# One hybrid attention and RWKV layer: the compressed branch's weights laid out as diagonal blocks of a 128x512 tile, in two parts

## The chip, the core and the metric

The kernel runs on one core of a Trainium2 chip. A core has several engines that run side by side, each with a queue of its own that it takes in order: TensorE (PE) multiplies matrices, its weight loads stand as PEld in the profile; VectorE (DVE), ScalarE (ACT) and GpSimd (POOL) work elementwise; SyncE (SP) starts most transfers, which 16 DMA engines carry out. Operands lie in SBUF with 128 partitions, and PE writes its results to PSUM. The metric is device time in microseconds (us) of one execution; less is better.

## What is computed

One layer on 512 tokens of 1024 features: an input projection, two mixers side by side (attention with three branches, and an RWKV7 recurrence), an output projection, and a feed-forward part. The change concerns the first of the three attention branches, the compressed one: keys and values of blocks of 32 tokens, one every 16, are each made into one compressed key and value, 31 of them. Cut to it, the reference reads:

```python
def query_block(q0):                      # 64 queries
    s_c = jnp.einsum('bqhgd,bnhd->bhgqn', qb, kc) - m[:, :, None, None] * d_c
    p_c = softmax_masked(s_c, d_c >= 0)
    o_c = jnp.einsum('bhgqn,bnhd->bqhgd', p_c, vc)     # n: 31 compressed values
    ...                                   # o_s: selected blocks, o_w: sliding window
    o = gb[..., 0:1] * o_c + gb[..., 1:2] * o_s + gb[..., 2:3] * o_w

# in the layer
x = x + jnp.concatenate([y_nsa, y_rwkv], axis=-1) @ w_out[l]
hidden = jnp.square(jax.nn.relu(rmsnorm(x, ln_ffn_g[l]) @ w_ff1[l]))
x = x + hidden @ w_ff2[l]
```

There are 8 query heads of 64 features, in two groups of four that share a key and value head.

## The kernel before

**Two-part numbers.** Most products are made from numbers split in two: a high part of the type fp32r (float32r), copied and rounded by ACT, and a low part, the remainder, subtracted by DVE (`split`, lines 311 and 312: `whi`, `wlo`). Products of such parts are single instructions of up to 512 columns. A plain product of two f32 operands stands in the trace as two matmul records.

**Units of attention.** The tokens lie in four tiles of 128. Attention is done in eight units, one for each pair of a key and value head g and a token tile i, g = 0 first, i from 0 to 3 in each. `attn_scores(i, g)` first makes the scores of the compressed branch for four heads (`pcs`, L1050), their exponentials, and divides them by their sum and multiplies by the gate; the result is `pcm`, 128 tokens by 4 heads x 32 blocks. Then it does the same with the two other branches over `w` = 128 (i + 1) keys (`sc`, products at L1072, DVE at L1076, ACT behind it, the tile is `P`). At the end PE transposes `pcm` (`pct`, L1089): row 32 h + n now holds the weights of head h for block n, with the tokens in the columns, and ACT copies it to SBUF (`pcT`, L1091). `attn_values(i, g)` goes through the key tiles of the two other branches in steps; a step transposes the four heads' weights (`pT`, L1108), splits them (`th` by ACT, L1112; `tl` by DVE, L1113) and multiplies the two parts with the values (`pv`, L1121 and L1125), 512 columns each, all into one PSUM tile. The first step also adds the compressed branch, one product for each head, in plain f32:

```python
if m == 0:
    for h in range(4):
        PE.matmul(pv[0:64, h * 128:(h + 1) * 128], VCM[:, g, h, :], pcT, start=False, stop=False)
```

`VCM[:, g, h, :]` is 128 x 64 and holds the compressed values in the rows 32 h to 32 h + 31 and zeros elsewhere (memset by POOL at L906), so that each product picks its head out of `pcT`. `tb` (L1129) and two adds then bring the unit's result into `YN`. The transposes `pct` and `pT` share a PSUM place "pb" with two buffers.

**What lies beside it.** The recurrence runs as other streams at the same time: `Tn` (L694) and `pz` (L681, L702) belong to the inverse of triangular matrices in blocks of 32, `QL` (L654) and `QD` (L963) are copies and splits on DVE, the chain over blocks of 64 tokens has the products `pp` and `puu` (64 columns), and at its end `py` (L752 to L755, 64 columns), from which `Sn` (L760), the new state, is made; `pty`, `rs_yo` and `Y` belong to the recurrence's output, `ptb` and `puu` to its preparation, `pq` transposes queries, and `kkn`, `mk` are elementwise products on the recurrence's keys. `wo_load` brings in `w_out`, the weights of the output projection, in two halves of eight tiles: each is loaded to one of two buffers (`wraw`, place 'wr'), copied by ACT (`whi`) and subtracted by DVE or POOL (`wlo`). The second half begins when the last unit's scores are made. `outproj` multiplies (`pa`, L332 to L334) as soon as the results of all units of a token tile are split. After that comes the feed-forward part (`pw`, `po`), which the change does not touch.

**What sets the order.** The streams are Python generators. Each yields the time that a step takes on PE and a delay, or a condition on what other streams have done; `merge` takes the stream of the best priority that is ready. The program written so is then handed to a scheduler that orders the instructions of each engine once more by its own model of their times. A changed instruction can therefore move others far from it, on all engines. Tiles in SBUF come from named places with a fixed number of buffers; a step waits for the buffer that it takes.

Of the kernel before, what the change touches and what calls it, by code (L numbers as in the profile page):

```python
# [16 lines left out]
# T tokens in NT tiles, D features in KD tiles; the rest orders the streams of work and their loads  # L17
T = 512
# [40 lines left out]
# places in SBUF: size of each in bytes, and how many  # L59
# [8 lines left out]
# columns of the constant array  # L68
# [46 lines left out]
def layer(ctx: ExitStack, tc: tile.TileContext, A, cst, out):  # L115
# [7 lines left out]
    # ------------------------------------------------------------- scheduling  # L123
    # Work is written as streams: a stream yields (time on the tensor engine, delay until what it
    # waits for is there), or a condition on the other streams, and the streams are merged by that.
# [30 lines left out]
    # ------------------------------------------------------------------ pools  # L156
# [24 lines left out]
    def cycle(*places):  # L181
        """Allocation that goes round some places."""
        k = [0]

        def f(shape, name, dt=F32):
            k[0] += 1
            return at(places[(k[0] - 1) % len(places)], shape, name, dt)
        return f
# [4 lines left out]
    # -------------------------------------------------------------- constants  # L193
# [15 lines left out]
    def gain_load(src, place):  # L209
        """Gains per feature, in all partitions."""  # L210
# [37 lines left out]
    # vectors that are used per feature, 128 features to a row  # L248
# [49 lines left out]
    # ---------------------------------------------------------------- helpers  # L298
    def rsqrt(v, n, key, p=128):
        """1/sqrt of a small array of positive numbers."""  # L300
# [6 lines left out]
    def split(raw, shape, hi=None, lo=None, eng=V):  # L307
        """A matrix in two parts, which add up to it exactly."""
# [27 lines left out]
    def norm_T(i, x_, gain, NH_, NL_, place, pool, raw=None):  # L336
        """Token tile i, normed, into the features' layout, in two parts."""
# [17 lines left out]
    # ------------------------------------------------------------ input norm  # L355
# [5 lines left out]
    def xk(k, i0=0, i1=NT):  # L361
        """The rows of a group of features, for tokens tiles i0 to i1."""
        return XH[k // 4][:, i0:i1, k % 4, :], XL[k // 4][:, i0:i1, k % 4, :]
# [6 lines left out]
    # =============================================================== RWKV  # L370
# [30 lines left out]
    # blocks of projected columns in the order of their use  # L401
# [6 lines left out]
    def turn_of(n):  # L408
        """A part of the input products waits for the one before it."""
# [10 lines left out]
    def raw_piece(p_):  # L420
        """A piece before it is split."""
# [6 lines left out]
    def piece(c0, h):  # L428
        """The next piece of the input weights; those after it are on their way."""
# [13 lines left out]
    def feat_cols(c0, use, halves=False):  # L443
        """Two tiles of 128 projected columns, features in the partitions."""
# [83 lines left out]
    def rw_prep(i):  # L528
# [49 lines left out]
        # products of keys with queries  # L578
# [26 lines left out]
    def rw_vals(i):  # L605
# [3 lines left out]
        # values, tokens in the partitions: odd heads in rows 0-63, even ones in rows 64-127  # L609
# [9 lines left out]
        # the bonus takes the place of the values in their other layout  # L619
# [25 lines left out]
    def rw_inv(i):  # L645
# [3 lines left out]
        # inverse of the triangular matrices: blocks of 32, merged from 2 up  # L649
# [162 lines left out]
    # =============================================================== NSA  # L812
# [7 lines left out]
    VCM = cp.tile([128, 2, 4, 64], F32, name="VCM")  # L820
# [3 lines left out]
    def nsa_consts():  # L824
        # gains of the keys, with those of the queries and the scale
# [7 lines left out]
    def tok_cols(c0, n, use):  # L833
        """Projected columns, tokens in the partitions."""
# [12 lines left out]
    def compress(kind, ckv):  # L847
        """Compressed keys (0) or values (1)."""
# [56 lines left out]
        else:  # L905
            G.memset(VCM, 0.0)  # L906
            for h in range(4):
                G.tensor_copy(VCM[32 * h:32 * h + 32, :, h, :], cm)
# [6 lines left out]
    def keys(b, kb):  # L915
        """Keys of branch b: normed, in two parts, transposed."""
# [55 lines left out]
    def nsa_in():  # L972
# [4 lines left out]
        def cmp_in(j, pa):  # L977
            """Each token's features with those of the next one below them."""
# [451 lines left out]
```

## Time and profile before

| | |
|---|---|
| device time, median of 3 runs | 816.68 us (814.18 to 823.08) |
| the profiled execution: span | 818.9 us, 18281 instructions; nothing is given outside the span |
| PE busy | 797.5 us, 97% of the span |
| PEld (weight loads, beside PE) busy | 684.4 us, 84% |
| DVE busy | 511.0 us, 62% |
| ACT busy | 395.9 us, 48% |
| POOL busy | 174.1 us, 21% |
| DMA | 62.00 MB, mean 76 GB/s |

The profiled execution is one run under the hardware profiler, recorded from its first to its last instruction. An engine's busy time counts the instructions that it carries out; PE's matmuls are pipelined, so a PE that is busy all the time is not one that runs at its peak. [...]

### The profile page before, as it was taken

Reading aid. Unit: us, or ns where it says so; the run is one execution under the profiler, and the core shown is the slowest. Engines: PE = TensorE matmul, PEld = TensorE weight load, DVE = VectorE, ACT = ScalarE, POOL = GpSimd, SP = SyncE. Lnnn points to the kernel's source line nnn. Section 1 sums busy time; section 2 is a strip of 40 time slices with the busy share of each in tenths; the row PEclk is TensorE's granted clock in tenths of the full one; section 3 lists DMA queues with packets and bytes.
Section 4 is the critical chain, followed back from the end, with each engine's and each line's share of the span. In section 5 each row is a group of like instructions: output and inputs, shape, how many; then the busy total and the mean of one; then the engine's idle time right before and its main releaser. Section 6 shows DMA issues by size and latency. Waiting matters only on the chain.

```text
span 818.9 us, 18281 instructions
## 1 busy us (share of the span) xinstructions
PE 797.5 (97%) x7357; PEld 684.4 (84%) x7357; DVE 511.0 (62%) x1157; ACT 395.9 (48%) x928; POOL 174.1 (21%) x176
## 2 busy tenths in 40 slices
PE   7999999999989999999999999999999999999998
PEld 5888888988878787887777889998888999978886
DVE  6344385674575399488764699986333799963333
ACT  6343334345353476569643564675332366663320
POOL 4002042312241252344320024310001323100000
PEclk9999999999975799599999999999999999999999
DMA  6741321120000000020134223314332343133212
GB/s 225 207 116 52 79 80 56 29 54 14 3 15 1 28 3 2 1 68 15 40 103 117 90 77 108 102 51 142 99 98 88 114 117 104 59 111 114 90 52 103
DMA packets 67338, 62.00 MB, mean 76 GB/s; under 512 B 6013, under 2 KB 53299, under 8 KB 67254
## 3 DMA queue, kind: packets, MB, share of 16 engines
q1 hardware_dynamic: 67254, 60.83, 24.9%
q8 instruction: 58, 0.95, 0.5%
q14 instruction: 26, 0.21, 0.1%
HBM read 58.72 MB, written 2.10 MB: 74 GB/s over the span
## 4 chain that ended last, share of the span: by engine, by line
PE 79%; DVE 11%; ACT 4%; DMA 3%; issue 2%; SPq 1%; POOL 0%; DVEq 0%; ACTq 0%; POOLq 0%
PE pa L332 7%; PE pa L333 7%; PE pa L334 7%; PE po L332 7%; PE po L333 7%; PE po L334 7%; PE pw L333 4%; PE pw L334 4%; PE pw L332 3%; PE sc L1072 3%; PE pg L586 2%; DVE wlo L312 2%; PE py L754 2%; PE py L752 2%; DMA wraw<-in_w_out_dram 2%
## 5 line engine op out<-in xcount | busy, mean ns | idle before, releaser
L311 ACT CAST whi<-wraw 128x512 fp32r<-128x512 f32 (+1 forms) x128 | 78.7, 622 | 141.5 <-PE po L333 29.1
L312 DVE TENSOR_TENSOR wlo<-wraw,whi 128x512 fp32r<-128x512 f32 (+1 forms) x120 | 86.2, 721 | 93.6 <-ACT whi L311 87.8
L332 PE MATMUL po<-whi 128*128 128x512 f32 x256 | 100.6, 394 | 1.6 <-DVE cc L1358 1.6
L333 PE MATMUL po<-wlo,whi 128*128 128x512 f32 x256 | 101.0, 395 | 0.0
L334 PE MATMUL po<-whi,wlo 128*128 128x512 f32 x256 | 100.7, 393 | 0.0
L333 PE MATMUL pw<-TT,whi 128*128 128x256 f32 x224 | 63.2, 282 | 0.0
L334 PE MATMUL pw<-TT,wlo 128*128 128x256 f32 x224 | 63.0, 281 | 0.0
L332 PE MATMUL pw<-TT,whi 128*128 128x256 f32 x224 | 62.5, 279 | 0.0
L332 PEld LDWEIGHTS po<-whi 128*128 128x128 f32 x256 | 48.0, 188 | 13.5 <-ACT whi L311 2.0
L334 PEld LDWEIGHTS po<-whi,wlo 128*128 128x128 f32 x256 | 48.1, 188 | 11.4
L333 PEld LDWEIGHTS po<-wlo,whi 128*128 128x128 f32 x256 | 48.1, 188 | 11.0
L332 PE MATMUL pa<-XH,whi 128*128 128x512 f32 (+1 forms) x144 | 53.6, 377 | 1.0 <-ACT XH L350 1.0
L333 PE MATMUL pa<-XL,whi 128*128 128x512 f32 (+1 forms) x144 | 54.4, 379 | 0.0
L334 PE MATMUL pa<-XH,wlo 128*128 128x512 f32 (+1 forms) x144 | 53.5, 374 | 0.0
L1086 POOL TENSOR_SCALAR P<-P,z 128x128 f32<-128x128 f32 (+3 forms) x32 | 35.6, 1122 | 77.9 <-DVE z L1035 35.5
L1288 POOL TENSOR_TENSOR ws<-wq 128x512 f32<-128x512 f32 x14 | 21.5, 1533 | 138.4 <-DMA wq<-in_w_ff_dram 123.4
L312 DVE TENSOR_TENSOR wlo<-ws,whi 128x512 fp32r<-128x512 f32 x56 | 48.1, 870 | 3.1 <-ACT whi L311 3.0
L311 ACT CAST whi<-ws 128x512 fp32r<-128x512 f32 x56 | 33.0, 618 | 34.8 <-PE pw L334 10.0
L312 DVE TENSOR_TENSOR wlo<-H,whi 128x512 fp32r<-128x512 f32 x32 | 22.1, 689 | 42.3 <-PE po L333 32.7
L334 PE MATMUL pw<-NH,wlo 128*128 128x256 f32 x168 | 47.0, 280 | 0.0
L333 PE MATMUL pw<-NL,whi 128*128 128x256 f32 x168 | 46.8, 279 | 0.0
L332 PE MATMUL pw<-NH,whi 128*128 128x256 f32 x168 | 46.8, 279 | 0.0
(319 smaller groups left out, 2109.8 us busy)
## 6 DMA issues: line engine op xcount, KB each, us to landing
wraw<-in_w_ff_dram SPq DMA_DIRECT2D x72, 256.0 KB
wq<-in_w_ff_dram SPq DMA_DIRECT2D x56, 256.0 KB
wraw<-in_w_in_dram SPq DMA_DIRECT2D x40, 256.0 KB
wraw<-in_w_in_dram SPq DMA_DIRECT2D x8, 268.0 KB
x<-in_x_dram SPq DMA_DIRECT2D x8, 256.0 KB
y<-in_x_dram SPq DMA_DIRECT2D x8, 256.0 KB
wraw<-in_w_out_dram SPq DMA_DIRECT2D x8, 256.0 KB
wraw<-in_w_out_dram SPq DMA_DIRECT2D x16, 128.0 KB
```

What stands on the lines that cost most here:

```text
L311: S.copy(hi, raw)
L312: eng.tensor_tensor(lo, raw, hi.bitcast(F32), op=ALU.subtract)
L332: PE.matmul(o_, l[0], r[0], start=first, stop=False)
L333: PE.matmul(o_, l[0], r[1], start=False, stop=False)
L334: PE.matmul(o_, l[1], r[0], start=False, stop=last)
L586: PE.matmul(pg[:, f], BK[ROW[e], 2 * f + c].rearrange("p a b -> p (a b)"), AR[c][ROW[e], f].rearrange("p a b -> p (a b)"), start=True, sto ...
L752: PE.matmul(py[ROW[1 - e], 1, f, :], AR[c][ROW[e], f, 1, :], S_[ROW[e], f, :], start=True, stop=False)
L754: PE.matmul(py[ROW[1 - e], 1, f, :], YL[e][c][:, f, 1 - e, :], uv, start=not q, stop=True)
L1072: PE.matmul(sc[:, h - h0, :], Qt[:, h, :], KT[br, g, hl].rearrange("p i t -> p (i t)")[:, 0:w], start=hl == 0, stop=hl == 1)
L1086: (G if (h, br) in SCG else V).tensor_scalar(P_[:, h, 0:w], P_[:, h, 0:w], z[:, h:h + 1], None, op0=ALU.mult)
L1288: G.tensor_tensor(s3, q[0][0], q[1][0], op=ALU.subtract)
```

## The change

The four plain products become two products of parts. `VCM` now holds the compressed values of a head in all four groups of 32 rows, its high part in columns 0 to 63 and its low part in columns 64 to 127. The weights take the shape of diagonal blocks: a tile `PCD` of 128 x 512 has the weights of head h in the rows 32 h to 32 h + 31 and the columns 128 h to 128 h + 127, and zeros elsewhere, one tile for the high part and one for the low. There are two such pairs, which the units take in turn; they are set to zero once, by POOL, and only the blocks are written after that: for each head one ACT copy of 32 rows by 128 from `pct` and one DVE subtract. The values' low part thus reaches the rows 64 to 127 of `pv`, which are added to the rows 0 to 63 at the unit's end as before. The program is also built with a smaller scratch area for DMA descriptors, 8192 bytes, and comments are dropped, so line numbers move by up to 12.

```diff
@@ -817,12 +817,15 @@
-    VCM = cp.tile([128, 2, 4, 64], F32, name="VCM")
+    VCM = cp.tile([128, 2, 2, 64], F32R, name="VCM")
+    PCD = [[cp.tile([128, 4, 128], F32R, name=f"PCD{n}{hl}") for hl in range(2)] for n in range(2)]
...
@@ -903,9 +906,14 @@
-            G.memset(VCM, 0.0)
+            v4 = at('cs', [128, 2, 64], "v4")
             for h in range(4):
-                G.tensor_copy(VCM[32 * h:32 * h + 32, :, h, :], cm)
+                G.tensor_copy(v4[32 * h:32 * h + 32], cm)
+            S.copy(VCM[:, :, 0, :], v4)
+            V.tensor_tensor(VCM[:, :, 1, :], v4, VCM[:, :, 0, :].bitcast(F32), op=ALU.subtract)
+            for n in range(2):
+                for hl in range(2):
+                    G.memset(PCD[n][hl].bitcast(F32), 0.0)
...
@@ -1087,16 +1095,19 @@
         PE.transpose(pct, pc.rearrange("p h n -> p (h n)"), ident)
-        pcT = at('cs', [128, 128], "pcT")
-        S.copy(pcT, pct)
-        AT[i, g] = P, pcT
+        pcd = PCD[UNITS.index((i, g)) % 2]
+        for h in range(4):
+            hr = slice(32 * h, 32 * h + 32)
+            S.copy(pcd[0][hr, h, :], pct[hr])
+            V.tensor_tensor(pcd[1][hr, h, :], pct[hr], pcd[0][hr, h, :].bitcast(F32), op=ALU.subtract)
+        AT[i, g] = P, pcd
...
@@ -1120,8 +1131,9 @@
                 if m == 0:
-                    for h in range(4):
-                        PE.matmul(pv[0:64, h * 128:(h + 1) * 128], VCM[:, g, h, :], pcT, start=False, stop=False)
+                    for hl in range(2):
+                        PE.matmul(pv, VCM[:, g].rearrange("p a b -> p (a b)"), pcd[hl].rearrange("p h t -> p (h t)"),
+                                  start=False, stop=False)
...
@@ -1413,7 +1425,7 @@
-    nc = _bacc.Bacc("TRN2", target_bir_lowering=False, num_devices=1)
+    nc = _bacc.Bacc("TRN2", target_bir_lowering=False, num_devices=1, dynamic_dma_scratch_size=8192)
```

The scheduler also orders the instructions anew. On PE the two programs run alike, but for a few products, up to the work around the first unit's values. There the program before has, in PE's order (line, operation, result <- operands, shape, and a count of like ones):

```order
L1050 MATMUL pcs<-KCT,QT 128x32 x4
L597 MATMUL ptb<-identr,BK 128x64 x8
L1121 MATMUL pv<-th,VH 128x512
L1124 MATMUL pv<-pcT,VCM 64x128 x4
L1072 MATMUL sc<-KT,QT 128x384 x2
L1108 MATMUL pT<-identr,P 128x128 x4
L743 MATMUL puu<-LV,QU 64x64 x8
L966 MATMUL pq<-identr,QD 128x128 x4
L1125 MATMUL pv<-tl,VH 128x512
```

and the changed one, at the same place of PE's order:

```order
L974 MATMUL pq<-identr,QD 128x128 x4
L1119 MATMUL pT<-identr,P 128x128 x4
L1132 MATMUL pv<-th,VH 128x512
L1135 MATMUL pv<-PCD_177,VCM 128x512
L1135 MATMUL pv<-PCD_178,VCM 128x512
L1137 MATMUL pv<-tl,VH 128x512
L1080 MATMUL sc<-KT,QT 128x384 x4
```

The unit's first step now stands in one piece, where scores and products of the recurrence stood between its parts. Further on the runs of `py` are cut otherwise too: before there are five runs of 20 or more from here on (24, 20, 24, 24, 24), after four (19, 24, 24, 24), each beside other work.

On DVE, in the work that lies before between 296 and 329 us, the program before has:

```order
L1076 ISA P,mn<-sc,CT_171 128x384
L1076 ISA mn 128x1
L779 TENSOR_TENSOR YY<-YY,rs_yo 128x512
L1076 ISA P,mn<-sc,CT_171 128x384
L1076 ISA mn 128x1
L1113 TENSOR_TENSOR tl<-pT,th 128x512 x2
L561 SCALAR_TENSOR_TENSOR kkn<-k,VEC,pb 128x128
```

and the changed one:

```order
L776 TENSOR_REDUCE var<-sqy 128x8
L1102 TENSOR_TENSOR PCD_180<-pct,PCD_179 32x128
L1084 ISA P,mn<-sc,CT_171 128x384
L1084 ISA mn 128x1
L1084 ISA P,mn<-sc,CT_171 128x384
L1084 ISA mn 128x1
L1124 TENSOR_TENSOR tl<-pT,th 128x512
L777 TENSOR_SCALAR var<-var 128x8
L1102 TENSOR_TENSOR PCD_180<-pct,PCD_179 32x128
L561 SCALAR_TENSOR_TENSOR kkn<-k,VEC,pb 128x128
```

Two of the new subtracts stand between DVE's part of the scores, a `tl` and the recurrence's keys, and the output of the recurrence (`var`, `YY`) comes later than it did.

On ACT, at the end of the attention, the program before has:

```order
L311 CAST whi<-wraw 128x512 x2
L1112 CAST th<-pT 128x512
L311 CAST whi<-wraw 128x512
L789 ACTIVATE Y_4012<-pty,VEC 128x128 x4
L311 CAST whi<-wraw 128x512 x2
L1129 COPY tb<-pv 64x512
L311 CAST whi<-wraw 128x512
L311 CAST whi<-YN 128x512 x2
```

and the changed one:

```order
L311 CAST whi<-wraw 128x512
L1123 CAST th<-pT 128x512
L1101 CAST PCD_179<-pct 32x128
L311 CAST whi<-wraw 128x512
L1101 CAST PCD_179<-pct 32x128
L1123 CAST th<-pT 128x512
L789 ACTIVATE Y_4022<-pty,VEC 128x128 x4
L1101 CAST PCD_179<-pct 32x128
L311 CAST whi<-wraw 128x512
L1141 COPY tb<-pv 64x512
L1123 CAST th<-pT 128x512
L1101 CAST PCD_179<-pct 32x128
```

The copies of the second half of `w_out` now alternate with `th` and with the new pieces. On PE eight steps of `pv` stand behind the last `py` before, fifteen after, and the bulk of the output projection begins only before the last two of them.

## Rows read from the trace of the kernel before

**Rows 1.** The page: 40 slices (tenths busy, PE clock) and the chain's shares.
```profile
PE   7999999999989999999999999999999999999998
DVE  6344385674575399488764699986333799963333
PEclk9999999999975799599999999999999999999999
...
PE 79%; DVE 11%; ACT 4%; DMA 3%; issue 2%; SPq 1%; POOL 0%; DVEq 0%; ACTq 0%; POOLq 0%
```
**Rows 2.** Stretches: length, PE, PEld, DVE, ACT, POOL, PE clock, DMA, GB/s.
```profile
230.00:280.00 50.00, 46.89 (x403) 40.08 (x405) 28.21 (x113) 25.70 (x91) 13.43 (x13) 0.59 0.05 16
296.00:329.00 33.00, 31.70 (x480) 24.84 (x478) 32.02 (x101) 22.72 (x66) 14.12 (x12) 1.00 0.01 2
325.00:350.00 25.00, 25.00 (x249) 21.02 (x249) 11.97 (x64) 14.81 (x55) 6.91 (x8) 0.66 0.00 1
356.00:380.00 24.00, 23.71 (x548) 19.79 (x546) 21.41 (x65) 19.88 (x58) 10.82 (x11) 1.00 0.23 69
410.00:420.00 10.00, 8.78 (x45) 6.59 (x44) 7.00 (x11) 5.11 (x10) 3.61 (x3) 0.83 0.19 53
420.00:440.00 20.00, 19.03 (x89) 15.15 (x89) 12.19 (x20) 8.39 (x17) 2.25 (x2) 1.00 0.56 167
```
**Rows 3.** The chain that ended last: start us, length us, what; the pv products.
```profile
269.84 1.90 PE pv L1124 x8
...
291.81 1.02 PE pv L1124 x8
...
410.98 1.90 PE pv L1124 x8
...
413.61 0.43 PE pv L1121
...
414.90 0.23 PE pv L1121
```
**Rows 4.** Timeline of ACT: start, length, line, operation.
```profile
401.16 0.27 ACT L1091 COPY pcT<-pct 128x128 f32<-128x128 f32 x1
```
**Rows 5.** Timeline of DVE between 258 and 260 us, in brackets its idle time.
```profile
258.35 0.42 DVE L760 TENSOR_TENSOR Sn<-py,Sn 128x256 f32<-128x256 f32 x1 [5.67 <-PE py L755]
258.69 0.42 DVE L963 TENSOR_TENSOR QD<-QR,QD 128x256 fp32r<-128x256 f32 x1
259.14 0.28 DVE L654 COPY QL<-GA 32x256 f32<-32x256 f32 x1
259.45 0.42 DVE L963 TENSOR_TENSOR QD<-QR,QD 128x256 fp32r<-128x256 f32 x1
```
**Rows 6.** Timeline of PE at the first fall; the stretch before the second.
```profile
234.16 1.07 PE L702 MATMUL pz<-Tn,QU 32*32 32x32 f32 x32 [3.11 <-DVE Tn L694]
...
326.00:329.00 3.00, 3.00 (x36) 2.13 (x34) 2.90 (x15) 2.31 (x10) 0.89 (x1) 1.00 0.00 0
```
**Rows 7.** The chain at the end of the attention: one step's parts, two loads.
```profile
414.46 0.45 PE pT L1108 x4
...
415.84 0.59 ACT th L1112
...
416.46 0.69 DVE tl L1113
...
419.91 3.92 DMA wraw<-in_w_out_dram
...
434.78 3.98 DMA wraw<-in_w_out_dram
```
**Rows 8.** Timeline of POOL: the memset of VCM and an idle time.
```profile
0.99 0.51 POOL L906 MEMSET VCM<- 128x512 f32 x1
...
6.24 0.55 POOL L302 TENSOR_TENSOR rs_yn<-vv,MH 128x1 f32<-128x1 f32 x1 [4.73 <-DVE vv L343]
```
**Rows 9.** The page's list of DMA queues: packets, MB, share of 16 engines.
```profile
q1 hardware_dynamic: 67254, 60.83, 24.9%
```

More of the change, by code (lines that the diff above doesn't have):

```diff
@@ L1098, in attn_values @@
         yield 0.0, 2.0
-        P, pcT = AT[i, g]
+        P, pcd = AT[i, g]
         pv = pz_([128, 512], "pv")
```

## The prediction

> **What bounds the kernel now.** I read the page first: PE is nearly full in every slice, DVE is full only between the fifteenth and sixteenth slice and again in the feed-forward part, and the granted clock dips in two places [rows 1]. All that the change touches lies between 235 and 440 us, so the next view was a table by stretch [rows 2]. It splits the attention into kinds. In 296 to 329 us DVE is busy for 32.02 of 33 us while PE, at 31.70, holds short narrow products: there DVE sets the pace. In 356 to 380 us DVE (21.41 of 24) and ACT (19.88) set it together. Elsewhere PE is what ends last. [...] A microsecond saved on PE therefore counts in the PE stretches, counts double at the lower clock, and counts for nothing from 296 to 329 us, where one added to DVE counts in full.
>
> **The products.** [...] The chain of waits holds six of the eight units (at 269.84, 291.81, 338.27, 380.17, 390.67 and 410.98 us), three at each level: 3 x (1.90 - 0.86) + 3 x (1.02 - 0.46) = 4.8 us off the path. The two others lie in the DVE stretch and in 356 to 380 us and count for nothing. **Term: -4.8**, between -3.4 (all six at the upper level) and -5.9 (all eight on the path).
>
> **The pieces on DVE.** One ACT copy of 0.27 us [rows 4] becomes four ACT and four DVE instructions of 32 rows by 128. No row shows such a subtract. Nearest is the 32-row copy QL: between two 128-row subtracts it takes 0.28 us, and the next one starts 0.76 us after the one ahead of it, where two of them in a row start 0.34 us apart [rows 5]. So a piece adds 0.42 us. The lower bound is 0.21 us, if its neighbours overlap it as they do each other.
>
> [...]
>
> I count the pieces that fall in DVE-bound time by the changed order: eight in the work of 296 to 329 us (two units), four to six in that of 356 to 380 us, where I let half count. 8 x 0.42 + 2 x 0.42 = 4.2 us. **Term: +4.2**, between 1.7 (8 x 0.21) and 6.7 (16 x 0.42). The ACT pieces add three times 0.27 us a unit at most; in 296 to 329 us ACT has 10 us free and hides them.
>
> **The falls of the clock.** The first follows a wait of PE for DVE (Tn) of 3.11 us [rows 6]. DVE's order up to that Tn gains one small instruction, the split of VCM, far ahead of it, and is otherwise unchanged, so the wait and the fall stay; the order behind it holds the same narrow products up to the first unit's, so its length stays too. The second came with no wait at all: from 326 to 329 us PE is busy 3.00 of 3.00 us [rows 6] with py, the 64-column products of the state, and the third directly behind another run of py. The order before has five runs of 20 or more py at the upper level; the clock fell after two. What came next differs: behind the second the clock rose after 17.0 us of 128-column scores and small transposes, behind the third after 3.4 us of 512-column products; I carry both lengths over to what stands behind a run in the changed order.
>
> [...]
>
> The changed order has four new runs of 19 to 24 (one shortened to 19, three whole); two are followed by narrow work, two by scores and pv of 384 to 512 columns. At two in five: 0.4 x (17.0 + 17.0 + 3.4 + 3.4) = 16.3 us at half clock against 20.4 now, and half of the difference is time. **Term: -2.0**, between -10.2 (no fall) and +10.2 (each of the four).
>
> **The tail.** Before, eight steps of pv follow the last run of py, and products of the output projection fill PE between them. In the changed order fifteen do, and the projection's bulk begins only before the last two. In the same stretch ACT's order alternates th with the eight whi of the second half of w_out. ACT takes its instructions in order, so a late load holds th, th holds tl, tl holds PE. Those loads come in pairs, 4.96 us a pair (three pairs from 419.91 to 434.78 us) [rows 7], 14.9 us for the eight if the first pair is there in time; PE has eight steps (pT 0.45, two pv of 0.23 us [rows 3, 7]) and about 1.6 us of others to do meanwhile, 8.9 us. That is 6 us of waiting at the worst. PE idles 1.22 us in 410 to 420 and 0.97 us in 420 to 440 us now [rows 2], partly for the same loads, which then come earlier. **Term: +2.0**, between -2.2 and +6.0.
>
> **What costs nothing.** Four memsets of PCD in place of one of VCM: 1.5 us more on POOL, which idles 4.73 us behind it [rows 8]; without that cover they would delay the first norm by as much. The smaller scratch area for DMA: every load comes on the queue q1, which uses a quarter of the engines' time [rows 9]; if loads slowed, the tail would show it first. The transposed weights pct now keep one of the two PSUM buffers "pb" until the fourth piece is done. If pT goes one at a time meanwhile, a step is 0.45 + 0.59 + 0.69 us in place of 0.91 [rows 3, 7], 0.8 us more, some 13 us for two steps in each unit; the changed order puts only one or two pT there with other work between, so I take 0 and keep it for the upper end.
>
> **Sum.** -4.8 + 4.2 - 2.0 + 2.0 = -0.6 us. The rows come from an execution with a span of 818.9 us; no row shows anything outside the span, and the median of the three runs is 2.2 us below it. 818.9 - 0.6 - 2.2 = 816.1 us.
>
> **Rivals.** *No falls behind py (faster).* If no run of py is followed by a fall, the third term is -10.2; with the tail as now, at 0: -4.8 + 4.2 - 10.2 = -10.8, 805.9 us. For it: three of five runs before had none. Against: the runs are whole in three places. Chance 0.22. *No first fall (faster).* Where PE waits a little less than 3.11 us, the 41.0 us at half clock go too, up to 20 us, 796 us; nothing in the order shortens that wait. Chance 0.05. *A paced tail (slower).* In the fifteen steps ahead of the projection PE waits for w_out through ACT, 6.0 us, and where one such wait comes near the 3.11 us of the first fall, the clock falls there as well: 1.7 to 8.5 us more, half of 3.4 and 17.0, middle 5.1. -4.8 + 4.2 + 0 + 6.0 + 5.1 = +10.5, 827.2 us. For it: ACT's order; against: PE waited there for 2.2 us only with the same loads. Chance 0.23. That the products do not become cheaper is excluded: their form is in [rows 3].
>
> **Chances and range.** A measurement of this kernel, whose three runs spread from 814 to 823 us, can tell about 1%, 8.2 us, from no change. The forecast, within that on both sides, has 0.50; the two faster rivals together 0.27, the slower one 0.23. The range goes from 805 us (the first rival) to 829 us (the third with a longer fall); what lies outside is the missing first fall and a serial pT.
>
> **What would show it.** [...] I am wrong if the later falls go or multiply, since that term is as wide as all others together.

## The result, and the profile after

The changed kernel takes 829.22 us (median of 4 runs, 828.2 to 831.34) against 817.92 us before (814.18 to 823.08): a ratio of 1.0138, 95% interval 1.0089 to 1.0188. The profiled execution has a span of 827.3 us at a mean clock of 0.959, before 818.9 us at 0.961. The clock is that granted to TensorE, as a share of full speed. Read in stretches of 1 us, it is 1.00 in 752 of the first 818 of the kernel before, 0.50 in 59 and between the two in 7 (748, 59 and 20 of 827 in the changed kernel); a 512-column product takes 0.23 us of the chain where it reads 1.00 (at 414.90 us) and 0.43 us where it reads 0.50 (at 413.61 us) [rows 3]. The two are called the upper and the lower level. Ratios, here and below, are of a version's runs at its higher clock: runs over 1.5% longer than its fastest one are left out of them (7 of 12 of the small chain that reads SBUF, 6 of 14 with the low pieces by POOL, 3 of 11 and 3 of 12 of alternating from SBUF and of the kernel before with pieces from SBUF, none of the kernel before), while the times in us are medians of all runs.

The page of the changed kernel, the rows that answer to [rows 1]:

```profile
PE   7999999999989989999889989999999999999998
DVE  6334476665577599688772589995333798963333
PEclk9999999999966889998799999999999999999999
...
PE 84%; DVE 9%; ACT 3%; DMA 2%; issue 1%; POOL 0%; SPq 0%; DVEq 0%; ACTq 0%; POOLq 0%
```

PE has new gaps in the fifteenth, the twentieth, the twenty-first and the twenty-fourth slice, and the clock is below 9 in six slices in place of four, and less deep. The table by stretch of the kernel before, for the whole attention and two parts of it (columns as in [rows 2]):

```profile
200.00:460.00 260.00, 252.92 (x3345) 206.50 (x3345) 172.26 (x522) 143.73 (x411) 77.82 (x72) 0.88 0.11 35
280.00:310.00 30.00, 29.50 (x661) 23.63 (x662) 23.65 (x78) 16.69 (x51) 11.59 (x12) 1.00 0.02 5
400.00:430.00 30.00, 28.61 (x195) 22.18 (x194) 20.29 (x37) 14.59 (x31) 7.88 (x5) 0.94 0.31 98
```

and of the changed kernel, with the stretch of the first fall of the clock:

```profile
200.00:460.00 260.00, 242.40 (x3257) 197.81 (x3257) 179.35 (x546) 148.72 (x424) 75.81 (x70) 0.88 0.10 31
230.00:280.00 50.00, 45.88 (x540) 39.73 (x539) 34.16 (x136) 30.89 (x109) 14.60 (x16) 0.69 0.05 15
280.00:310.00 30.00, 26.63 (x445) 22.07 (x436) 24.11 (x70) 13.56 (x38) 13.62 (x12) 0.83 0.02 6
400.00:430.00 30.00, 23.59 (x100) 16.44 (x99) 24.75 (x46) 20.78 (x43) 8.63 (x6) 0.80 0.33 105
```

From 200 to 460 us PE idles for 17.6 us in place of 7.1, at the same mean clock, 0.88. In these two executions the 10.5 us are the loss: over the whole span PE's busy time fell by 1.7 us (795.8 after 797.5), and the span grew by 8.4 (the medians lie 11.3 us apart). What PE waited for there, in the changed kernel (engine, line, releaser: us in total, times, longest):

```profile
PE pv L1135 <- DVE PCD L1102: 4.3, 2, 3.4
PE pv L1132 <- DVE YN L1147: 3.4, 3, 1.6
PE pz L702 <- DVE Tn L694: 3.1, 1, 3.1
PE pty L784 <- DVE YY L779: 1.4, 1, 1.4
PE pT L1119 <- DVE tl L1124: 1.1, 3, 0.6
PE pv L1132 <- ACT th L1123: 0.9, 3, 0.4
```

The wait for Tn was there before [rows 6]. The first row is new: the products wait for the low pieces. Why the pieces are late is seen in the timeline of one unit, the second, whose weights PE transposed at 289.65 us; first ACT, then DVE, then PE:

```profile
290.16 0.26 ACT L1101 CAST PCD<-pct 32x128 fp32r<-32x128 f32 x1 [1.02 <-PE pct L1097]
...
291.62 0.26 ACT L1101 CAST PCD<-pct 32x128 fp32r<-32x128 f32 x1
...
294.73 0.26 ACT L1101 CAST PCD<-pct 32x128 fp32r<-32x128 f32 x1
...
297.55 0.26 ACT L1101 CAST PCD<-pct 32x128 fp32r<-32x128 f32 x1
```

```profile
290.44 0.28 DVE L1102 TENSOR_TENSOR PCD<-pct,PCD 32x128 fp32r<-32x128 f32 x1 [0.18 <-ACT PCD L1101]
...
293.57 0.28 DVE L1102 TENSOR_TENSOR PCD<-pct,PCD 32x128 fp32r<-32x128 f32 x1
...
296.65 0.29 DVE L1102 TENSOR_TENSOR PCD<-pct,PCD 32x128 fp32r<-32x128 f32 x1
...
298.03 2.90 DVE L575 SCALAR_TENSOR_TENSOR AR<-kkn,PP 128x256 f32<-128x256 f32 x2
300.85 0.68 DVE L1124 TENSOR_TENSOR tl<-pT,th 128x512 fp32r<-128x512 f32 x1
...
301.64 0.30 DVE L1102 TENSOR_TENSOR PCD<-pct,PCD 32x128 fp32r<-32x128 f32 x1
```

```profile
298.13 0.49 PE L1135 MATMUL pv<-PCD,VCM 128*128 128x512 f32 x1
302.00 0.50 PE L1135 MATMUL pv<-PCD,VCM 128*128 128x512 f32 x1 [3.37 <-DVE PCD L1102]
```

The eight pieces are eight steps of a chain: each subtract needs its copy, and no copy starts before the subtract of the piece ahead of it has ended. At each step the piece stands in a queue behind other work; the last one behind two AR of 2.90 us together, a `tl` and a reciprocal. So 2.2 us of pieces take 12.3 us. From the transpose to the last subtract it is 11.1, 12.3, 8.9, 10.2, 4.5, 19.2, 13.8 and 9.1 us in the eight units, 11.1 on average, where the one copy of before had read `pct` after 1.0 on average. All this time `pct` keeps its PSUM buffer.

The program says the same: in the changed one a copy waits for DVE, while in a version whose pieces are made from a copy in SBUF (below) it does not. ACT's second piece in the changed program, and the second to fourth in the other, with the waits that stand at them:

```
L1101 CAST PCD_177<-pct 32x128 [waits DVE_49]
L1103 CAST PCD_177<-pcT 32x128 x3
```

Whether the hardware needs these waits was not shown: no run has the alternating order from PSUM without them.

### The profile page after: what moved, and what is told of

It reads as the page before. It is cut to its first block, busy times and chain, and to the rows that moved or that the text cites. A ratio compares the mean times of both kernels' runs of the same rounds, so it can differ in the third digit from the quotient of the medians.

```text
span 827.3 us, 18246 instructions
## 1 busy us (share of the span) xinstructions
PE 795.8 (96%) x7309; PEld 682.9 (83%) x7309; DVE 522.2 (63%) x1190; ACT 405.5 (49%) x953; POOL 175.4 (21%) x179
## 4 chain that ended last, share of the span: by engine, by line
PE 84%; DVE 9%; ACT 3%; DMA 2%; issue 1%; POOL 0%; SPq 0%; DVEq 0%; ACTq 0%; POOLq 0%
PE pa L332 8%; PE pa L333 8%; PE pa L334 8%; PE po L332 7%; PE po L333 7%; PE po L334 7%; PE pw L333 5%; PE pw L334 5%; PE pw L332 5%; PE sc L1080 2%; PE pg L586 2%; PE py L754 2%; PE py L752 2%; PE pT L1119 2%; PE pd L681 1%
## 5 line engine op out<-in xcount | busy, mean ns | idle before, releaser
L1300 POOL TENSOR_TENSOR ws<-wq 128x512 f32<-128x512 f32 x14 | 21.4, 1529 | 137.8 <-DMA wq<-in_w_ff_dram 123.1
```

What stands on the lines that cost most here:

```text
L1300: G.tensor_tensor(s3, q[0][0], q[1][0], op=ALU.subtract)
```

## The experiments

Each is timed beside the kernel before on the same chip in five rounds; ratios are to that kernel, with the 95% interval. "Kept" is the mean time of eight units from the transpose to the end of the last read of `pct`, "done" the mean time from the transpose to the end of the last piece, both from the traces; idle PE is span less PE busy in the profiled execution. After each edit the scheduler orders all engines anew, so that no two versions, the twins below included, differ by the edit alone; what holds a buffer also shapes that order, and the two can't be told apart here. That an arbitrary new order is not what costs is seen from all versions together: by their ratios seven that let the buffer go within 2.5 us and need no late piece early (five of the table, the POOL and the DMA version) lie between 0.9899 and 1.0022, and the five that keep one for over 9 us between 1.0093 and 1.0301.

| version | kept, us | done, us | products at | idle PE, us | ratio |
|---|---|---|---|---|---|
| before | 1.0 | - | first step | 21.4 | 1 |
| changed | 11.1 | 11.1 | first step | 31.5 | 1.0138 |
| products at the last step | 9.6 | 9.6 | last step | 32.0 | 1.0093 |
| pct in the scores' place | 12.0 | 12.0 | first step | 33.3 | 1.0106 |
| before, pieces on top | 12.1 | 12.1 | unused | 34.9 | 1.0241 |
| before, pieces on top, from SBUF | 1.0 | 4.7 | unused | 24.3 | 1.0012 |
| small chain, reads PSUM last | 15.3 | 6.2 | first step | 36.1 | 1.0301 |
| small chain, reads SBUF | 1.1 | 6.2 | first step | 26.2 | 1.0022 |
| alternating from SBUF | 1.3 | 18.4 | first step | 28.5 | 1.0103 |
| alternating from SBUF, products last | 1.5 | 19.6 | last step | 24.7 | 0.9951 |
| copies first, then subtracts | 4.5 | 4.5 | first step | 27.7 | 1.0030 |
| padded | 4.2 | 4.2 | first step | 23.6 | 0.9955 |
| pieces from SBUF | 0.9 | 5.4 | first step | 24.3 | 0.9943 |
| pieces left out | 1.4 | - | first step | 21.0 | 0.9899 |

**The pieces left out.**

```diff
-        for h in range(4):
-            ...
+        S.copy(pcd[0][:, 0, :], pct)
```

Expected: 

> The changed kernel with its two 512-column products, but the weights' eight pieces are left out: one ACT copy of 128x128 takes the weights into the first block of the high tile, and nothing is split (the compressed branch is left wrong). Late pieces: the two waits of PE for PCD (4.3 us in all) and the waits for YN behind them go, what is left is the gain of the products, 4.8 us: a ratio to the kernel before of 0.990 to 0.998. New order alone (any rearrangement by the scheduler costs what this one did, mostly by falls of the clock): 1.005 to 1.02. Held buffer (the transposed weights keep a PSUM buffer for up to 20 us): the copy lets it go at once, so as for late pieces.

Measured: 0.9899 (0.9879 to 0.9919), 811.68 us. The products alone are worth some 8 us, and PE idles no more than before. The loss comes with the pieces; a new order without them, which this version has too, does not bring it.

**The weights copied to SBUF first.**

```diff
+        pcT = at('cs', [128, 128], "pcT")
+        S.copy(pcT, pct)
         for h in range(4):
             hr = slice(32 * h, 32 * h + 32)
-            S.copy(pcd[0][hr, h, :], pct[hr])
-            V.tensor_tensor(pcd[1][hr, h, :], pct[hr], ...)
+            S.copy(pcd[0][hr, h, :], pcT[hr])
+            V.tensor_tensor(pcd[1][hr, h, :], pcT[hr], ...)
```

Expected: 

> The changed kernel, but ACT first copies the transposed weights to SBUF in one instruction, and the eight pieces are made from there, so that the PSUM buffer comes free at once. Held buffer: the loss goes, a ratio of 0.99 to 1.00 to the kernel before, and PE waits less for th and tl. Late pieces: PE still waits for the last piece, some 4 us, and one ACT instruction a unit is added: 1.010 to 1.020. New order alone: no telling, within 1.005 to 1.02.

Measured: 0.9943 (0.9921 to 0.9965), 815.78 us. The expectation did not foresee that this edit also ends the alternation. The view by tile of `PCD`, from 249.5 to 255 us of this version, the first unit's pieces (start of the first and of the last behind the durations):

```profile
L1103 ACT CAST PCD<-pcT x4: 282/294/297, 251.2 to 252.2; 32x128 fp32r<-32x128 f32 x4
L1104 DVE TENSOR_TENSOR PCD<-pcT,PCD x4: 268/281/286, 253.0 to 254.0; 32x128 fp32r<-32x128 f32 x4
```

Four copies, then four subtracts in a row. So the same work with one instruction more turned a loss of 1.4% into a gain of 0.6%; whether by the free buffer or by the early pieces stays open here.

**The products at the unit's last step.**

```diff
-                if m == 0:
+                if last:
                     for hl in range(2):
                         PE.matmul(pv, VCM[:, g].rearrange("p a b -> p (a b)"), ...
```

Expected: 

> The changed kernel, but the two products with PCD are written behind the high part's product of a unit's last step instead of its first, so that the pieces have the time of the unit's steps. Late pieces: the waits of PE for PCD fall under 1 us in all and most of the 10.5 us of idle PE goes: 0.990 to 1.003. Held buffer: pct still keeps its buffer for 4 to 20 us, so 1.008 to 1.02. New order alone: 1.005 to 1.02.

Measured: 1.0093 (1.0063 to 1.0122), 826.58 us. PE no longer waits for `PCD` at all; its longest waits from 200 to 460 us are

```profile
PE pg L586 <- ACT LV L640: 6.1, 1, 6.1
PE pz L702 <- DVE Tn L694: 3.1, 1, 3.1
PE pv L1132 <- ACT th L1123: 2.0, 4, 0.8
```

and it idles as long as before this edit. The 4.3 us of waits for the pieces were the visible part only. No `pct` stands in the longest wait: ACT came late to LV because it had itself waited 5.06 us for DVE's part of the scores:

```profile
297.10 0.61 ACT L1087 ACTIVATE P<-P,mn 128x384 f32<-128x384 f32 x1 [5.06 <-DVE mn L1084]
```

**Spread ahead of the transpose** (the tile `PCM` is zeroed once, and one buffer of the place 'cs' is given up for it).

```diff
-        V.tensor_tensor(pc, pc, bc(zc.unsqueeze(2), [128, 4, 32]), op=ALU.mult)
+        V.tensor_tensor(PCM.rearrange("p a b n -> p (a b) n")[:, 0:16:5, :], pc, bc(...), op=ALU.mult)
...
-        PE.transpose(pct, pc.rearrange("p h n -> p (h n)"), ident)
+        for h in range(4):
+            PE.transpose(pct[:, h, :], PCM[:, h].rearrange("p h n -> p (h n)"), ident)
...
+        S.copy(pcd[0], pct)
+        V.tensor_tensor(pcd[1], pct, pcd[0].bitcast(F32), op=ALU.subtract)
```

Expected: 

> The changed kernel, but the weights are spread before the transpose: the last DVE operation on them writes into the diagonal of a padded tile of zeros, four transposes of 128x128 in place of one give the whole block tile in PSUM, and one ACT copy and one DVE subtract of 128x512 make both parts, in place of four and four pieces. DVE has 8 x 0.69 = 5.5 us of it in place of 32 x 0.28 = 9.2 us, and one handoff in place of eight; PE gets three transposes more a unit, about 8 x 0.3 = 2.4 us. Late pieces: 0.990 to 1.000. Held buffer: as late pieces. New order alone: 1.005 to 1.02.

Measured: 0.9955 (0.9936 to 0.9974), 815.33 us, as expected of late pieces or a held buffer.

**Four copies, then four subtracts, from PSUM.**

```diff
         for h in range(4):
             hr = slice(32 * h, 32 * h + 32)
             S.copy(pcd[0][hr, h, :], pct[hr])
+        for h in range(4):
+            hr = slice(32 * h, 32 * h + 32)
             V.tensor_tensor(pcd[1][hr, h, :], pct[hr], ...)
```

Expected: 

> The changed kernel with its eight pieces a unit still read from PSUM, but written as four ACT copies and then four DVE subtracts, so that DVE is handed the tile once and no ACT copy waits for a DVE subtract. Same instructions, same source. Alternation (each ACT copy of a piece waits for the subtract of the piece before it, eight handoffs through two queues in order): the loss goes, 0.992 to 1.000. Load (the 32 subtracts' 9.2 us of DVE time cost as much): stays at 1.008 to 1.018. Held buffer alone: pct is still kept until the last subtract, so it follows the measured time from the transpose to that subtract; if that stays over 5 us in most units, 1.005 or more.

Measured: 1.0030 (1.0005 to 1.0055), 820.61 us. The same instructions in another order of two loops give back most of the loss, a little less than expected. Their load is thus not the cause.

**The transposed weights in the scores' place.**

```diff
-        pct = pb_([128, 128], "pct")
+        pct = pa_([128, 128], "pct")
```

Expected: 

> The changed kernel with the transposed weights in a PSUM buffer of the scores' place (pa) instead of the place of pT (pb); the pieces alternate as before. Held buffer, as far as it is pT that lacks one: the loss goes, 0.992 to 1.002. Alternation with late pieces: PE still waits for PCD, 1.005 to 1.02; the scores of the next unit lack a buffer instead, which may cost the same again.

Measured: 1.0106 (1.0076 to 1.0137), 826.3 us. It is not that pT in particular lacks a buffer; a buffer of the scores' place kept for 12.0 us costs about the same. This run alone leaves both theories.

**The pieces on top of the kernel before, unused.** `PCD` and the loop of pieces stand behind the copy of before; the four plain products stay.

```diff
         S.copy(pcT, pct)
+        pcd = PCD[UNITS.index((i, g)) % 2]
+        for h in range(4):
+            hr = slice(32 * h, 32 * h + 32)
+            S.copy(pcd[0][hr, h, :], pct[hr])
+            V.tensor_tensor(pcd[1][hr, h, :], pct[hr], ...)
```

Expected: 

> The kernel before with its four plain products and its copy of the weights, and the changed kernel's eight alternating pieces made on top, from PSUM, with nobody who uses them (the smaller scratch area too). Held buffer: as much as the change lost, without the gain of the products: 1.012 to 1.022. Late pieces that PE waits for: nobody waits here, so only the load on DVE and ACT is left, 0.998 to 1.008. Load: 1.005 to 1.011.

Measured: 1.0241 (1.0206 to 1.0275), 837.35 us, more than any theory gave. Nobody needs these pieces, so no product can be late for them. Its twin reads `pcT` in place of `pct`:

Expected: 

> The kernel before with its four plain products, and the eight pieces a unit made on top and used by nobody, now from the copy of the weights in SBUF, so that the PSUM buffer is free after the first copy. Its twin, which makes them from PSUM, had 1.0241. Held buffer: only the load of the pieces is left, 1.000 to 1.008. Load of the pieces, or the new order: as its twin, 1.018 or more.

Measured: 1.0012 (0.9981 to 1.0042), 821.22 us. For the kernel with the old products the pair rules out the load and the late pieces: the eight pieces cost 1 us as work, not clear of noise, and 18.8 us more (0.0229 of 819; 16.1 between the medians) when they alternate on a PSUM tile and keep it for 12.1 us. Which of the two, the alternation or the kept buffer, the next pair asks.

**A small chain that keeps the buffer, and its twin.** Pieces from SBUF, and beside them

```diff
+        za, zb = small(4, "za"), small(4, "zb")
+        for h in range(4):
+            S.copy(za[:, h:h + 1], zb[:, h - 1:h] if h else pcT[:, 0:1])
+            V.tensor_tensor(zb[:, h:h + 1], za[:, h:h + 1], (pct if h == 3 else pcT)[:, 0:1], op=ALU.add)
```

where the twin has `pcT` in all four.

Expected: 

> The version with the pieces made from a copy in SBUF (0.9943), and beside it a chain of eight tiny instructions (128x1) that alternate between ACT and DVE; the last of them reads the transposed weights in PSUM, so that their buffer is kept until the chain ends. The pieces themselves come early. Held buffer: most of the loss comes back though no piece is late, 1.005 to 1.015. Late pieces, or the load of the pieces: only the tiny instructions are added, some 4 us of ACT and DVE at most, 0.994 to 1.001, and no different from its twin, whose chain does not read PSUM.

Expected of the twin: 

> The twin of the one before: the same eight tiny instructions in the same chain, but the last one reads the copy in SBUF, so the PSUM buffer comes free at the first copy. All theories but a general cost of handoffs: 0.994 to 1.001. If any chain that alternates between the two engines costs by its handoffs alone, as much as its twin, 1.005 or more.

Measured: 1.0301 (1.0258 to 1.0345), 844.81 us, against 1.0022 (0.9981 to 1.0062). The twin's runs scatter from 816 to 832 us; the median, 829.25 us, is 1.011 of before, and every one is below the fastest run of the other, 839.17. One operand of one column, read from PSUM late, costs 1.9 to 2.8%, with the order that the scheduler makes around it, though `PCD` is complete after 6.2 us in both. Not all of it is idle time: the held version idles 9.9 us longer than the profiled execution of its twin (36.1 after 26.2) and has a mean clock of 0.941 in place of 0.951, in a span that is 15.2 us longer. The twin itself is above its expectation, 0.8% over the version without a chain (0.9943), so the small chain was not free. In the held version the read is also seen to stop PE, in the view by tile of `zb` (the instruction, then who waited for the tile: us, times):

```profile
L1108 DVE TENSOR_TENSOR zb<-za,pct x8: 126/144/155, 269.9 to 440.5; 128x1 f32<-128x1 f32 x8
...
  PE pT L1125: 1.4, 1
```

**Alternating pieces with a free buffer.** From SBUF, made to alternate by a bias of zeros that DVE makes from the piece before:

```diff
+            if h:
+                V.tensor_scalar(zt[:, h:h + 1], pcd[1][:, h - 1, 0:1].bitcast(F32), 0.0, None, op0=ALU.mult)
+                S.activation(pcd[0][hr, h, :], pcT[hr], AF.Identity, bias=zt[hr, h:h + 1])
```

Expected: 

> The pieces are made from a copy in SBUF, so the PSUM buffer is free at once, but they are made to alternate as in the changed kernel: each ACT piece after the first takes its bias (zeros) from a tiny DVE instruction that reads the low piece before it. Pieces late, buffer free. Late pieces and alternation: PE waits for PCD as in the changed kernel, 1.008 to 1.018. Held buffer: 0.994 to 1.002, the 0.9943 and up to 4 us for three tiny DVE instructions a unit.

Measured: 1.0103 (1.0062 to 1.0144), 826.31 us: against the held buffer as the only cause. It is not the changed kernel with a free buffer, though: the pieces are done after 18.4 us in place of 11.1, and an ACT piece with its bias takes 397 ns in place of 257. PE waits for `PCD` only 0.2 us in it; the scheduler has put the products later, the first at 284.8 us, where the changed kernel has it at 272.4:

```profile
L1142 PE MATMUL pv<-PCD,VCM x16: 392/487/796, 284.8 to 417.6; 128*128 128x512 f32 x16
```

With the products at the last step in addition:

Expected: 

> The version with a free buffer whose pieces alternate (1.0103), with the two products written behind the high product of a unit's last step. If it was the late pieces that PE needed: 0.996 to 1.003, near the version with the small chain that holds nothing (1.0022). If it is the alternation itself, by which ACT and DVE wait for each other in their queues: 1.007 to 1.013.

Measured: 0.9951 (0.9927 to 0.9974), 815.32 us, though the pieces are done after 19.6 us. So pieces that alternate cost nothing that is seen here as long as no product needs the last one early and they keep no buffer; the early need shows in the order of the work, not as a wait for the piece.

**Versions meant to be faster.** The low pieces by POOL, from the copy in SBUF (`G.tensor_tensor` for `V.tensor_tensor`):

Expected: 

> The changed kernel with one ACT copy of the transposed weights to SBUF, the high pieces by ACT from there, and the low pieces by POOL in place of DVE: no alternation, no held buffer, and DVE gets none of the new work. Alternation or held buffer: 0.988 to 0.996, at or below the 0.9943 of the version with DVE; if POOL's subtracts are slow, PE waits for PCD and it is 0.995 to 1.000. Load on DVE: the lower end, near the 0.990 of the version without pieces.

Measured: 0.9936 (0.9911 to 0.9960), 814.46 us. A subtract takes POOL 0.45 us, and PE did not wait for it:

```profile
L1104 POOL TENSOR_TENSOR PCD<-pcT,PCD x32: 444/452/794, 251.5 to 414.4; 32x128 fp32r<-32x128 f32 x32
```

The blocks carried by DMA:

```diff
+        S.copy(hc, pct)
+        V.tensor_tensor(lc, pct, hc.bitcast(F32), op=ALU.subtract)
+        for h in range(4):
+            hr = slice(32 * h, 32 * h + 32)
+            nc.sync.dma_start(pcd[0][hr, h, :].bitcast(F32), hc[hr].bitcast(F32))
+            nc.sync.dma_start(pcd[1][hr, h, :].bitcast(F32), lc[hr].bitcast(F32))
```

Expected: 

> A version meant to be faster than both: one ACT copy and one DVE subtract of 128x128 make the high and the low part of the transposed weights, and eight small DMAs a unit (32x128) carry them to the diagonal blocks. DVE gets 8 x 0.28 us in place of 32, PSUM is free after two instructions, and the DMAs have 12 us or more until the products. 0.988 to 0.995; if the loads of w_out, which stand behind these DMAs in SP's queue, come late, 0.996 to 1.01 with waits of ACT's whi for DMA in the tail.

Measured: 0.9947 (0.9922 to 0.9972), 815.45 us. PE waits for the blocks twice, the wait as the profile names it:

```profile
PE pv L1138 <- DMA PCD<-hc: 2.0, 2, 1.2
```

By their ratios five versions beat both kernels, with intervals that overlap (0.9936 to 0.9955); none reaches the 0.9899 without the pieces.

**The scratch area alone.**

```diff
-    nc = _bacc.Bacc("TRN2", target_bir_lowering=False, num_devices=1)
+    nc = _bacc.Bacc("TRN2", target_bir_lowering=False, num_devices=1, dynamic_dma_scratch_size=8192)
```

Expected: 

> The kernel before with the smaller scratch area for DMA descriptors alone; its instructions and their order are the same. All theories: 0.998 to 1.002. If loads slowed, more than 1.003.

Measured: 0.9983 (0.9959 to 1.0007), 817.93 us: no part in it.

## Why the prediction was wrong, point by point

The forecast was 816.1 us within 805 to 829, no change the likeliest; measured were 829.2 us, a slower kernel.

**The step that failed** is the one under "What costs nothing", that `pct` keeps a buffer of "pb" until the fourth piece is done. It was seen, priced at 0.8 us a serial step and 13 us at the upper end, and then taken at 0, because the changed order puts one or two pT into that time. What was wrong is the time itself: the pieces were priced as work on DVE, and never as a chain of eight handoffs through two queues. That the copies wait for the subtracts stands in the changed program, and that each instruction waits its turn behind others was known of DVE from its busy time (32.02 of 33 us from 296 to 329 us [rows 2]). In its place the runs showed pieces that take 11.1 us from end to end, and two costs that such late pieces can have. Laid out as a square of four, the ratios are

| | products at the first step | at the last step |
|---|---|---|
| buffer kept (pieces alternate on PSUM) | 1.0138 | 1.0093 |
| buffer free (pieces alternate on SBUF) | 1.0103 | 0.9951 |

With the products at the last step, keeping the buffer costs 1.4%; with the buffer free, needing the pieces at the first step costs 1.5%, of pieces still later than the changed kernel's; both together cost 1.9% over neither. Either one is thus enough, and taking away one alone makes the changed kernel only 0.3 to 0.5% faster, which the intervals do not tell from nothing. The first pair of twins, with no need at all, puts the kept buffer at 2.3%, the second at 1.9 to 2.8%.

The serial pT that the prediction priced is there to see. In the last two units `pct` is kept from 393.88 to 407.66 and from 412.94 to 422.08 us, and in that time PE waits at three steps with pT for the `tl` of the step just before it, as it would with one buffer:

```profile
404.56 0.66 PE L1119 MATMUL pT<-identr,P 128*128 128x128 f32 x4 [0.16 <-DVE tl L1124]
...
414.65 0.66 PE L1119 MATMUL pT<-identr,P 128*128 128x128 f32 x4 [0.34 <-DVE tl L1124]
...
421.89 0.66 PE L1119 MATMUL pT<-identr,P 128*128 128x128 f32 x4 [0.62 <-DVE tl L1124]
```

Counted over all 40 steps of the traces, pT begins only after the `tl` just before it in 21 steps of the changed kernel and in 20, 19 and 27 of the three other versions that keep a buffer of "pb" for over 9 us; it does in 15 of the kernel before and in 12 to 18 of all other versions, the one with `pct` in the scores' place among them. Six steps more, at the prediction's 0.8 us, would be some 5 us, an estimate. With the prediction's own upper price of 13 us the sum would have given 829.1 us, the measured time almost to the digit; that would have been luck in part, since products and clock came out otherwise than their terms too.

**The products** had -4.8 us, to -5.9 at most: a unit's eight records of before, 1.02 us together at a clock of 1.00 (291.81 us) and 1.90 at 0.50 (269.84 and 410.98 us), against two products of 0.23 or 0.43 us [rows 3]. Without pieces the kernel gains 8.3 us (6.6 to 9.9), more than the term allowed; with pieces from SBUF the new products are 5.7 us faster than the old ones (0.9943 against 1.0012), with some 2 us on either side of each, so the term may also have been right. Their durations came as read, as the chain that ended last in the changed kernel shows (start, length; the first unit's two products and one of the third's, with two late pieces of the second unit on the path):

```profile
272.56 0.46 PE pv L1135 x2
...
293.57 0.28 DVE PCD L1102
...
301.64 0.30 DVE PCD L1102
...
319.42 0.23 PE pv L1135
```

That is the 0.23 us a product of [rows 3]. So the price of a product was right. The count of units on the path does not explain 8.3 us, since all eight make 5.9; what the rest comes from stays open, and the new order of that version may be part of it.

**The pieces as work** had +4.2, between 1.7 and 6.7: from the version without them to that with pieces from SBUF it is 3.6 us (0.0044), from the kernel before to that with unused ones 1.0 us; the size was about right, the second figure below its range but not clear of it. A subtract takes 286 ns; four in a row start 0.31 us apart, not 0.42 (the rows from 253.0 to 254.0 above): each starts after the end of the one ahead, since 0.31 is more than the median of 0.281. The 0.42 us was the author's estimate from the copy QL among its neighbours [rows 5].

**The clock** had -2.0, between -10.2 and +10.2. Its lengths are those of [rows 2]: in stretches of 1 us the kernel before shows 41.0, 17.1 and 3.4 us at 0.50, from 233, 329 and 410 us on. Two in five was an estimate from that one trace. With 0.50 as the lower level, the time there is twice the missing clock times the span: 2 x 0.039 x 818.9 = 63.9 us before, 2 x 0.041 x 827.3 = 67.8 us after, of which half is time: +2.0. The first fall did follow the same wait for Tn of 3.1 us, but its stretch has 31.0 us at the lower level (0.69) in place of 41.0, and others came behind it. In both traces PE's waits of 3.11 us before and of 3.13 and 3.37 us after have a fall that begins in them or within 1 us of their end, and the next longest, of 2.25 and 2.26 us, have none; a wait of a little less than 3.11 us, on which the rival without a first fall rests, stands in neither.

**The tail** had +2.0, and its rival of 827.2 us comes near the measured time, but not by its mechanism. From 400 to 430 us PE idles 6.4 us in place of 1.4; what it waits for there are `YN`, `PCD`, `th` and `tl` of units that come late. No wait for w_out stands among PE's rows of the changed kernel, and ACT, by which the rival would have it come, waits for w_out only 1.9 us there, 0.8 at the longest. The rival's other half, a fall of the clock in that stretch, did come: 0.80 in place of 0.94.

**What costs nothing** held for the scratch area (0.9983) and for the memsets: the stretch up to 200 us was not longer (PE busy 193.5 us of it, before 193.4).

What stays open: by which instructions the rest of the kept buffer's cost becomes time, and how much of it is the order that the scheduler makes around it. Few waits name `pct`; a likely reason, not shown, is that the program's order already has the later transposes behind its release. The cost shows as PE idle time, 31 to 36 us in the five versions that keep a buffer for over 9 us, 20 to 26 us in those with a free one and no early need of late pieces, and in the held small chain as a lower clock besides. Open too is why the padded version (0.9955) and that with copies first (1.0030) differ at nearly the same kept time; DVE is busy 7.7 us less in the padded one (513.7 after 521.4), which no run takes by itself.

## What to carry to other kernels

A small tile that two engines read in turn should be taken out of PSUM by one instruction, and cut up from SBUF: here one more copy of 0.27 us a unit was worth 2.0% (1.0138 to 0.9943). When one instruction is replaced by several on two engines, count the handoffs and what stands in each queue ahead of them, not only the durations, and ask which buffer is kept until the last. Where a result is made late, let the step that needs it come last among steps that commute: with the buffer free that was worth 1.5% (1.0103 to 0.9951), with the buffer kept nothing that is clear of noise (1.0138 to 1.0093).

## What the runs showed of the hardware

A run of four DVE subtracts that start at partitions 0, 32, 64 and 96 took 1.2 us, and POOL needed 0.45 us for what DVE did in 0.28. PE's clock fell in other places in the changed kernel (in stretches of 1 us from 203, 234, 258, 285, 302, 381, 398, 405, 422 and 487 us on) than before (from 233, 329, 410 and 817 us on), while the time at the lower level stayed between 52 and 72 us in most versions (mean clocks 0.968 and 0.957, reckoned as above); the held small chain, at 0.941, had 99.6 us of it, and the profiled execution with the low pieces by POOL, which keeps no buffer, 98.0 us at the same mean.
